# Low parts of weights kept in DRAM after their first use and loaded for the second

## The chip, the cores and the metric

The kernel runs on one core of a Trainium2 chip. The core has a matrix engine (TensorE, PE in the rows; its weight loads are PEld), VectorE (DVE), ScalarE (ACT), GpSimd (POOL) and SyncE (SP), which here only issues DMA transfers (SPq). They work side by side and wait for one another by semaphores. The metric is the time on the device in microseconds (us), smaller is better.

## The reference

One step of a hybrid decoder layer over 1088 token columns: 1024 of a prompt and 64 of samples (8 sequences of 8 tokens), with width 1024, in fp32. Cut to what matters:

```python
h = rms_norm(x, g1)
z = h @ w_in                      # 1024 -> 3*512 + 2*256 + 256 columns
y = concat(rwkv7(z[:1536]), rg_lru(z[1536:2048]), s5(z[2048:]))
x = x + y @ w_out
q = rms_norm(x, g2) @ wq          # cross-attention, 4 heads, 256 memory tokens
x = x + attend(q, mem @ wk, mem @ wv) @ wo
x = x + swiglu(rms_norm(x, g3))   # hidden 2816
y = rms_norm(x, gf)
```

Here `rwkv7` is a recurrence over tokens with a 64 x 64 state for each of 8 heads, `rg_lru` a gated linear recurrence behind a short convolution, and `s5` a linear recurrence with complex states.

## The kernel before, in words

**Products in two parts.** Both operands of a large product are split into a high part (rounded to the matmul's format, fp32r) and a low part (what the rounding left off). `mm3` (L173 to L179) makes three matmuls for each block of 128 of the depth: high weight by high input (L177), high weight by low input (L178), low weight by high input (L179).

**Weights.** `load_w` (L145) brings one tile of 128 x 1024 numbers (512 KB) into `wr`; `wsplit` (L150) has ACT write the high part `wh` (L75, the helper `act`) and POOL subtract it from the raw tile, which gives the low part `wl` (L81, the helper `tt`):

```python
    hi = wp.tile(shape, F32R, name="wh", tag="wh")
    lo = wp.tile(shape, F32R, name="wl", tag="wl")
    act(hi, raw)
    tt(lo, raw, f32(hi), OP.subtract, G)
```

The pool `wp` has two buffers each for `wr`, `wh` and `wl`, so a tile's load waits until the tile two before it has been used up.

**Halves of the columns.** The columns are worked in two parts, `hf` 0 (576 columns, the samples among them) and `hf` 1 (512 columns). The 16 tiles of `w_in` that belong to the RWKV and RG-LRU branches (0 to 15) are loaded and split for half 0 in `zmix` (L750) and `lru` (L865, L922), and loaded and split again for half 1. Tiles 16 and 17 (S5) serve both halves in one go. The 8 tiles of `wo` are loaded in `project` (L1375), which `w_o` (L1538) calls for each half.

**What lies beside them.** Half 0 of `w_in` runs from about us 100 to 340. Half 1 lies at us 340 to 640, mixed with the recurrence of RWKV for half 0 (`Chunks`: chunk states `SV`, matmuls `pp` and `ch`, the triangular inverse with `Wu`, `Xu` and `tm`), whose operands go through DRAM (`ar`, `bk`, `inv_d`, `inv_e` and others). `w_o` of half 0 lies in the stretch 640 to 1094, `w_o` of half 1 at 1094 to 1149, with norm work of half 0 for the SwiGLU blocks beside it on DVE (`late_norm`: `h`, `bt`, `bl`, `b`). The SwiGLU blocks take the rest, from 1149 to 1904; their first weights (`in_w_up`) come into `wX` buffers that older work must leave first.

**Order.** All transfers are issued from one engine (`ld = nc.sync.dma_start`, SP), in one order; one that must wait for its buffer holds back all that stand behind it. Sections with a priority (`pr`) and a scheduler that goes by its own model of times set the order of the instructions on each engine, once, when the program is built; the engines then follow it.

Of the kernel before, what the change touches and what calls it, by code (L numbers as in the profile page):

```python
# [7 lines left out]
F32 = mybir.dt.float32  # L8
F32R = mybir.dt.float32r
# [5 lines left out]
P = 128  # L15
# [40 lines left out]
def body(tc, I, O, dbg=None):  # L56
# [7 lines left out]
    def pool(name, stack, side=None, space=None, bufs=1):  # L64
        kw = dict(name=name, bufs=bufs)
        if space is not None:
            kw['space'] = space
        if space != DRAM:
            kw['reuse_waits'] = "tile"
        if side is not None:  # L70
            kw['side'] = side
        return stack.enter_context(tc.tile_pool(**kw))

    def act(out, in_, f=AF.Copy, **kw):
        return S.activation(out, in_, f, **kw)  # L75
# [4 lines left out]
    def tt(out, a, b, op, eng=None):  # L80
        return (eng or V).tensor_tensor(out, a, b, op=op)  # L81
# [6 lines left out]
    def f32(ap):  # L88
        return ap.bitcast(F32)
# [11 lines left out]
    ld = nc.sync.dma_start  # L101

    cst = pool("cst", es)
    dram = pool("dram", es, space=DRAM)
    wp = pool("wp", es, bufs=2)
# [36 lines left out]
        G.memset(kc[:, i:i + 1], x)  # L142
    k_rms, k_gn, k_ln30, k_tiny, k_hpi, k_zero = (kc[:, i:i + 1] for i in range(6))

    def load_w(ap, shape=(P, 8, P)):  # L145
        raw = wp.tile(list(shape), F32, name="wr", tag="wr")
        ld(raw, ap)
        return wsplit(raw, list(shape))

    def wsplit(raw, shape):  # L150
        hi = wp.tile(shape, F32R, name="wh", tag="wh")
# [3 lines that stand above are left out]
        return hi, lo  # L155
# [55 lines left out]
    for hf, hp in ((0, hpA), (1, hpB)):  # L211
        w = W[hf] + (8 if hf == 0 else 0) + 1
# [13 lines left out]
    def mmt():  # L226
        return psD.tile([P, 512], F32, name="mm", tag="mm", bufs=2)
# [47 lines left out]
    def win(hf, w, evac):  # L275

        wh, wl = w
        for c0, n in GH[hf]:
            pt = mmt()
            mm3(pt[:, :n], lambda k: (wh[:, k, :], wl[:, k, :]), hx(hf, c0, n), 8)  # L280
            evac(c0, n, min(n, 512 - c0), pt[:, :n], RS[hf][:, 1 + c0:1 + c0 + n])
# [8 lines left out]
    for i, (a, b, mus) in enumerate(LORA1):  # L290
        w = b - a
        raw = load_lora1(i) if i else first_w
# [109 lines left out]
    wh, wl = split_w(2, 0)  # L402
    for hf in range(2):
        for c0, n in NG[hf]:
            pt = smt()
            s = 2 if c0 else 1
# [145 lines left out]
    d = 1  # L552
    while d < P:
        n = [P, 8, d]
# [14 lines left out]
    raw = wp.tile([P, 1024], F32, name="wr", tag="wr")  # L569
# [8 lines left out]
    for hf in range(2):  # L578
        for p in range(4):
            for kind in range(3):  # L580
                t = lp.tile([P, W[hf]], F32, name="wag", tag=("lmu", "wag")[(p + kind) % 2], bufs=2)
                for c0, n in GX[hf]:
                    pt = smt()
                    m = slice(P * p, P * p + P)
# [15 lines left out]
    for m in range(2):  # L600
        w = load_w(I['w_in'][16 + m])
# [16 lines left out]
    def e(name, tag="t"):  # L618
        return ep.tile([P, 592 if tag == 'zb' else 576], F32, name=name, tag=tag, bufs=EB[tag])
# [97 lines left out]
    for hf in range(2):  # L717
        for m in range(2):
            yo = sp.tile([P, W[hf]], F32, name="yo", tag="yo", bufs=2)
            for c0, n in GX[hf]:  # L720
                c = slice(OFF[hf] + c0, OFF[hf] + c0 + n)
                pts = []
                for half in (1, 0):
                    pt = smt()
                    o = 256 * half + P * m
# [14 lines left out]
    def zmix(hf, mt, tag):  # L740
        zb, z = e("zb", "zb"), e("z" + tag, tag)
        if hf:
            V.tensor_copy(zb[:, 0:1], zlast[:, mt:mt + 1])
        else:
            V.memset(zb[:, 0:1], 0.0)
        om, mu = omu[:, mt:mt + 1], v_('mu_rkv', mt)

        def ev(c0, n, m, pt, rs):
            tt(zb[:, 1 + c0:1 + c0 + n], pt, rs, OP.mult)
        win(hf, load_w(I['w_in'][mt]), ev)  # L750
        act(z[:, :512], zb[:, 1:513], AF.Copy, scale=om)
        if hf == 0:
            act(bview(z[:, 512:576]), sview(zb[:, 513:585]), AF.Copy, scale=om)
        stt(z[:, :512], zb[:, :512], mu, z[:, :512], OP.mult, OP.add)
        if hf == 0:
            V.tensor_copy(zlast[:, mt:mt + 1], zb[:, 512:513])
            zs = bview(z[:, 512:576])
            stt(zs, zb[:, 513:585].rearrange("p (b t) -> p b t", t=9)[:, :, 0:8], mu, zs, OP.mult, OP.add)
        return z[:, :W[hf]]
# [91 lines left out]
    def lru(hf, m):  # L851
        w = W[hf]
# [8 lines left out]
        def evac_x(c0, n, k, pt, rs):  # L861
            tt(ext[:, 3 + c0:3 + c0 + k], pt[:, :k], rs[:, :k], OP.mult)
            if n > k:
                tt(exs[:, :, 3:11], sview(pt[:, k:]), sview(rs[:, k:]), OP.mult)
        win(hf, load_w(I['w_in'][12 + m]), evac_x)  # L865
        if hf:
            ld(O['conv'][m, :, 0, :], ext[:, 512:515])
        else:
# [19 lines left out]
        s, ns = sp4[:, m:m + 1], nsp4[:, m:m + 1]  # L888
# [29 lines left out]
        def evac_g(c0, n, k, pt, rs):  # L918
            tt(gz[:, c0:c0 + k], pt[:, :k], rs[:, :k], OP.mult)
            if n > k:  # L920
                tt(bview(gz[:, 512:576]), sview(pt[:, k:]), sview(rs[:, k:]), OP.mult)
        win(hf, load_w(I['w_in'][14 + m]), evac_g)  # L922
        gz = gz[:, :w]
        act(gz, gz, AF.Gelu_apprx_tanh)
        tt(gz, gz, hs, OP.mult)
# [446 lines left out]
                stt(h, X[self.hf][:, kt, lo:hi], v_(gname, kt), rs, OP.mult, OP.mult)  # L1372
                put(kt, h)

    def project(w, src, hf, evac, behind=None):  # L1375

        for mt in range(8):
            wh, wl = load_w(w[mt])
            for c0, n in GX[hf]:
                pt = mm_[0]()  # L1380
                mm3(pt[:, :n], lambda k: (wh[:, k, :], wl[:, k, :]),
                    lambda k: (src[k][0][:, c0:c0 + n], src[k][1][:, c0:c0 + n]), 8)
                if behind:
                    behind()
                evac(mt, c0, n, pt[:, :n])
# [62 lines left out]
    OA = [None, None]  # L1448
# [77 lines left out]
    late_norm = []  # L1526

    def w_o(hf):


        nm = Norm(hf)
        put = residual(hf, nm)

        def ev(mt, c0, n, pt):
            put(mt, c0, n, pt)
            if c0 + n == W[hf]:
                ld(x_d[hf][:, mt], X[hf][:, mt])
        project(I['wo'], OA[hf], hf, ev, late_norm.pop(0) if late_norm else None)  # L1538
        return nm

    def slot(hf, i, name):
# [564 lines left out]
```

## Time and profile before

| what | value |
|---|---|
| time, median of 3 runs (lowest to highest) | 1897.87 us (1897.86 to 1900.61) |
| profiled execution, own time | 1905.55 us |
| its span from first to last instruction | 1903.4 us |
| granted TensorE clock, mean over the span | 0.961 of full speed |
| busy: PE, DVE, ACT, POOL | 1780.8, 1108.9, 786.6, 696.0 us (94%, 58%, 41%, 37%) |
| HBM read, written | 170.47 MB, 56.23 MB |

The span is the profiled execution alone, and 2.2 us of its time lie around it. Busy time counts each engine's instructions by themselves, so the shares add up to more than 100%. The shares are means over stretches that have different limits. The chain that ended last is followed back from the last instruction to what released it at each step; where it stays on one engine, no other engine was waited for.

### The profile page before, as it was taken

The page shows a single profiled execution, that of the slowest core. Times are in us where ns is not written, and L with a number is a line of the kernel's source. Part 1 is how long each engine was busy: PE and PEld are TensorE (multiplying, and loading weights), DVE is VectorE, ACT ScalarE, POOL GpSimd, SP SyncE. Part 2 cuts the span into 40 slices and gives each one's busy share as a digit, 9 for nine tenths or more (in the row PEclk, how much of TensorE's full clock was granted, in tenths as well). Part 3 has the DMA queues.
Part 4 walks back from the last instruction along what each step waited for, and adds up shares of the span by engine and source line. Part 5 has one row for each costly group of instructions (what it writes and reads, how often), then busy time and mean ns, then how long its engine had stood idle before and what let it go on. Part 6 is the DMA issues. An engine that isn't in the chain of part 4 may idle for free.

```text
span 1903.4 us, 34672 instructions
## 1 busy us (share of the span) xinstructions
PE 1780.8 (94%) x13664; PEld 1617.9 (85%) x13664; DVE 1108.9 (58%) x2273; ACT 786.6 (41%) x1460; POOL 696.0 (37%) x513
## 2 busy tenths in 40 slices
PE   6998888998998889999999989999999999999997
PEld 6877887777877778897887968999999999999997
DVE  7763767797779454746755588633333333744435
ACT  8542443453434533534554355433333333311114
POOL 3311323434443423232221344744444443422235
PEclk9999998798999979999999998999999999999998
DMA  5037465436564743236553333322222223723102
GB/s 165 30 114 147 123 158 145 138 96 177 152 160 128 233 144 91 67 123 232 170 188 117 115 129 102 117 74 80 80 74 74 86 77 97 272 92 92 56 1 95
DMA packets 192146, 228.95 MB, mean 120 GB/s; under 512 B 80048, under 2 KB 128560, under 8 KB 191568
## 3 DMA queue, kind: packets, MB, share of 16 engines
q1 hardware_dynamic: 191984, 226.75, 39.4%
q8 instruction: 107, 1.75, 0.4%
q14 instruction: 55, 0.45, 0.1%
HBM read 170.47 MB, written 56.23 MB: 119 GB/s over the span
## 4 chain that ended last, share of the span: by engine, by line
PE 62%; DVE 12%; DMA 5%; ACT 2%; issue 2%; POOL 1%; SPq 1%; DVEq 0%; ACTq 0%; POOLq 0%
PE mm L177 17%; PE mm L179 17%; PE mm L178 17%; DMA AR<-ar 1%; PE pp L1052 1%; DVE bl L81 1%; DVE tm L81 1%; DVE Wu L81 1%; DVE Y L78 1%; DVE h L78 1%; DMA fg<-g 1%; DVE X L81 1%; PE ss L1499 1%; ACT L75 1%; PE ch L1124 1%
## 5 line engine op out<-in xcount | busy, mean ns | idle before, releaser
L81 POOL TENSOR_TENSOR wl<-wr,wh 128x1024 fp32r<-128x1024 f32 x104 | 257.5, 2477 | 459.0 <-ACT wh L75 413.3
L177 PE MATMUL mm<-HH,wh 128*128 128x256 f32 (+2 forms) x576 | 180.0, 313 | 11.8 <-DVE gz L81 4.6
L81 DVE TENSOR_TENSOR X<-X,mm 128x288 f32<-128x288 f32 (+2 forms) x200 | 100.5, 512 | 137.3 <-PE mm L179 136.4
L179 PE MATMUL mm<-gh,dl 128*128 128x288 f32 (+2 forms) x560 | 178.5, 319 | 0.0
L177 PE MATMUL mm<-gh,dh 128*128 128x288 f32 (+2 forms) x560 | 178.2, 318 | 0.0
L178 PE MATMUL mm<-gl,dh 128*128 128x288 f32 (+2 forms) x560 | 178.1, 318 | 0.0
L179 PE MATMUL mm<-HH,wl 128*128 128x256 f32 (+2 forms) x576 | 176.5, 307 | 0.0
L178 PE MATMUL mm<-HL,wh 128*128 128x256 f32 (+2 forms) x576 | 175.0, 304 | 0.0
L178 PE MATMUL mm<-bl,st 128*128 128x256 f32 (+1 forms) x596 | 172.2, 289 | 2.6 <-DVE bl L81 2.6
L75 ACT ACTIVATE wh<-wr 128x1024 fp32r<-128x1024 f32 (+1 forms) x105 | 110.3, 1051 | 154.4 <-PE mm L178 74.9
L179 PE MATMUL mm<-bh,st 128*128 128x256 f32 (+1 forms) x596 | 172.1, 290 | 0.6 <-POOL st L81 0.6
L177 PE MATMUL mm<-bh,st 128*128 128x256 f32 (+1 forms) x596 | 171.2, 289 | 0.8 <-ACT bh L75 0.7
L177 PE MATMUL mm<-bh,X 128*128 128x256 f32 (+1 forms) x580 | 165.7, 288 | 0.6 <-DVE p L81 0.5
L178 PE MATMUL mm<-bl,X 128*128 128x256 f32 (+1 forms) x580 | 166.2, 287 | 0.0
L179 PE MATMUL mm<-bh,X 128*128 128x256 f32 (+1 forms) x580 | 165.5, 287 | 0.0
L81 DVE TENSOR_TENSOR gy<-gy,mm 128x288 f32<-128x288 f32 (+1 forms) x130 | 56.7, 436 | 164.9 <-PE mm L179 164.5
L177 PEld LDWEIGHTS mm<-HH,wh 128*128 128x128 f32 x576 | 114.6, 199 | 20.0 <-issue 10.6
L81 POOL TENSOR_TENSOR dl<-wr,dh 128x512 fp32r<-128x512 f32 x44 | 64.6, 1503 | 163.5 <-ACT dh L75 143.4
L178 PEld LDWEIGHTS mm<-HL,wh 128*128 128x128 f32 x576 | 114.7, 199 | 5.1 <-issue 2.8
L179 PEld LDWEIGHTS mm<-HH,wl 128*128 128x128 f32 x576 | 114.5, 199 | 4.4 <-issue 2.2
L178 PEld LDWEIGHTS mm<-bl,st 128*128 128x128 f32 x596 | 113.3, 190 | 2.8 <-DVE bl L81 2.8
L179 PEld LDWEIGHTS mm<-bh,st 128*128 128x128 f32 x596 | 113.4, 190 | 0.8 <-POOL st L81 0.8
(498 smaller groups left out, 5125.1 us busy)
## 6 DMA issues: line engine op xcount, KB each, us to landing
wr<-in_w_in SPq DMA_DIRECT2D x34, 512.0 KB, 4.0
wX<-in_w_up SPq DMA_DIRECT2D x56, 256.0 KB, 2.7
wr<-in_w_down SPq DMA_DIRECT2D x22, 512.0 KB, 4.1
wr<-in_w_out SPq DMA_DIRECT2D x16, 512.0 KB, 4.7
wr<-in_wq SPq DMA_DIRECT2D x16, 512.0 KB, 3.5
kvb<-in_ck SPq DMA_DIRECT2D x32, 256.0 KB, 4.5
kvb<-in_cv SPq DMA_DIRECT2D x32, 256.0 KB, 4.6
wr<-in_wo SPq DMA_DIRECT2D x16, 512.0 KB, 3.5
```

The source lines that it names most:

```text
L75: return S.activation(out, in_, f, **kw)
L78: return V.scalar_tensor_tensor(out, a, s, b, op0=o0, op1=o1)
L81: return (eng or V).tensor_tensor(out, a, b, op=op)
L177: paced(TE.matmul(out, wh, xh, start=first and k == 0, stop=False, **kw))
L178: paced(TE.matmul(out, wh, xl, start=False, stop=False, **kw))
L179: paced(TE.matmul(out, wl, xh, start=False, stop=last and k == n - 1, **kw))
L1052: mi = TE.matmul(pvs[h][:, i, j], BK[o, i, j].rearrange("p a t -> p (a t)"), AR[o, i, h, j].rearrange("p a t -> p (a t)"), start=True, sto ...
L1124: mi = TE.matmul(ch[OWN[h], 0, i], AR[:, i, h, j, 0, :], SV[:, i, h, j, :], start=i == 0, stop=True, skip_group_check=True)
L1499: TE.matmul(sc[32 * h:32 * h + 32, :256], qp[:, 2 * h + dt, :], kb[:, dt, :], start=dt == 0, stop=dt == 1)
```

## The change

`load_w` takes a key. The first load of a tile with a key makes both parts as before, and the low part is then stored to a DRAM buffer of its own by a transfer of 512 KB. The second load of the same key brings the raw tile, has ACT make the high part, and loads the low part from that buffer by another transfer of 512 KB; the subtraction on POOL is not made. Keys are given to the 16 tiles of `w_in` and the 8 tiles of `wo`. So 24 subtractions on POOL go, and 24 stores and 24 loads are added, 12.6 MB each way, all issued by SP. From `load_w` on, line numbers are up to 12 higher than before.

```diff
--- before.py
+++ after.py
@@ -142,10 +142,22 @@
         G.memset(kc[:, i:i + 1], x)
     k_rms, k_gn, k_ln30, k_tiny, k_hpi, k_zero = (kc[:, i:i + 1] for i in range(6))
 
-    def load_w(ap, shape=(P, 8, P)):
+    lows = {}
+
+    def load_w(ap, shape=(P, 8, P), key=None):
+
         raw = wp.tile(list(shape), F32, name="wr", tag="wr")
         ld(raw, ap)
-        return wsplit(raw, list(shape))
+        if key in lows:
+            hi, lo = (wp.tile(list(shape), F32R, name=n, tag=n) for n in ("wh", "wl"))
+            act(hi, raw)
+            ld(f32(lo), lows.pop(key))
+            return hi, lo
+        hi, lo = wsplit(raw, list(shape))
+        if key:
+            lows[key] = dram.tile(list(shape), F32, name="lo_%s%d" % key)
+            ld(lows[key], f32(lo))
+        return hi, lo
 
     def wsplit(raw, shape):
         hi = wp.tile(shape, F32R, name="wh", tag="wh")
@@ -747,7 +759,7 @@
 
         def ev(c0, n, m, pt, rs):
             tt(zb[:, 1 + c0:1 + c0 + n], pt, rs, OP.mult)
-        win(hf, load_w(I['w_in'][mt]), ev)
+        win(hf, load_w(I['w_in'][mt], key=('in', mt)), ev)
         act(z[:, :512], zb[:, 1:513], AF.Copy, scale=om)
         if hf == 0:
             act(bview(z[:, 512:576]), sview(zb[:, 513:585]), AF.Copy, scale=om)
@@ -862,7 +874,7 @@
             tt(ext[:, 3 + c0:3 + c0 + k], pt[:, :k], rs[:, :k], OP.mult)
             if n > k:
                 tt(exs[:, :, 3:11], sview(pt[:, k:]), sview(rs[:, k:]), OP.mult)
-        win(hf, load_w(I['w_in'][12 + m]), evac_x)
+        win(hf, load_w(I['w_in'][12 + m], key=('in', 12 + m)), evac_x)
         if hf:
             ld(O['conv'][m, :, 0, :], ext[:, 512:515])
         else:
@@ -919,7 +931,7 @@
             tt(gz[:, c0:c0 + k], pt[:, :k], rs[:, :k], OP.mult)
             if n > k:
                 tt(bview(gz[:, 512:576]), sview(pt[:, k:]), sview(rs[:, k:]), OP.mult)
-        win(hf, load_w(I['w_in'][14 + m]), evac_g)
+        win(hf, load_w(I['w_in'][14 + m], key=('in', 14 + m)), evac_g)
         gz = gz[:, :w]
         act(gz, gz, AF.Gelu_apprx_tanh)
         tt(gz, gz, hs, OP.mult)
@@ -1372,10 +1384,10 @@
                 stt(h, X[self.hf][:, kt, lo:hi], v_(gname, kt), rs, OP.mult, OP.mult)
                 put(kt, h)
 
-    def project(w, src, hf, evac, behind=None):
+    def project(w, src, hf, evac, behind=None, name=None):
 
         for mt in range(8):
-            wh, wl = load_w(w[mt])
+            wh, wl = load_w(w[mt], key=name and (name, mt))
             for c0, n in GX[hf]:
                 pt = mm_[0]()
                 mm3(pt[:, :n], lambda k: (wh[:, k, :], wl[:, k, :]),
@@ -1535,7 +1547,7 @@
             put(mt, c0, n, pt)
             if c0 + n == W[hf]:
                 ld(x_d[hf][:, mt], X[hf][:, mt])
-        project(I['wo'], OA[hf], hf, ev, late_norm.pop(0) if late_norm else None)
+        project(I['wo'], OA[hf], hf, ev, late_norm.pop(0) if late_norm else None, 'o')
         return nm
 
     def slot(hf, i, name):
```

The first place is SP's order in `w_o` of half 1, before: `wr<-in_wo` are raw tiles of `wo` (the last is tile 7), `wX` are buffers for the SwiGLU weights, `x` the stores of the result.

```order
L1776 DMA wX<-in_w_up 128x512
L1537 DMA x_3543<-X 128x512
L147 DMA wr<-in_wo 128x1024
L1537 DMA x_3543<-X 128x512
L147 DMA wr<-in_wo 128x1024
L1776 DMA wX<-in_w_up 128x512
L1537 DMA x_3543<-X 128x512
L147 DMA wr<-in_w_up 128x1024
L1776 DMA wX<-in_w_up 128x512
```

The same place with the change, where `lo_o_...` are the DRAM buffers of the low parts, the last (11116) that of tile 7, the one before (11049) that of tile 6:

```order
L1788 DMA wX<-in_w_up 128x512
L1549 DMA x_3575<-X 128x512
L154 DMA wl<-lo_o_10982 128x1024
L150 DMA wr<-in_wo 128x1024
L1549 DMA x_3575<-X 128x512
L1788 DMA wX<-in_w_up 128x512
L154 DMA wl<-lo_o_11049 128x1024
L150 DMA wr<-in_w_up 128x1024
L1549 DMA x_3575<-X 128x512
L154 DMA wl<-lo_o_11116 128x1024
L1788 DMA wX<-in_w_up 128x512
L150 DMA wr<-in_w_up 128x1024
```

The load of a low part stands behind the load of its raw tile, and between the two stand, for tiles 6 and 5, stores of `x`, the next raw tile or a `wX` load.

The second place is SP's order ahead of the first chunk of half 0, where the recurrence's operands `BK` and `AR` are read back from DRAM, before:

```order
L147 DMA wr<-in_w_in 128x1024
L846 DMA bv_114<-zz 128x576
L962 DMA Xu<-inv_d_2059 128x1024
L870 DMA out_conv<-exs 128x8x3
L995 DMA Xs<-sd_d 64x64
L1033 DMA BK<-bk_110 128x4x128
L1035 DMA AR<-ar_108 64x4x128 x2
L1036 DMA vt<-v_112 128x4x64
```

With the change, with low parts of `w_in` (`lo_in_...`):

```order
L150 DMA wr<-in_w_in 128x1024
L154 DMA wl<-lo_in_2079 128x1024
L150 DMA wr<-in_w_in 128x1024
L858 DMA bv_114<-zz 128x576
L154 DMA wl<-lo_in_2155 128x1024
L882 DMA out_conv<-exs 128x8x3
L974 DMA Xu<-inv_d_2059 128x1024
L1007 DMA Xs<-sd_d 64x64
L1045 DMA BK<-bk_110 128x4x128
L1047 DMA AR<-ar_108 64x4x128 x2
```

Two low parts and one more raw tile have come ahead of the `AR` loads, and stay in the same queue.

The third place is POOL's order about us 500, where `zk` is made from `f` for the operands of half 1, before:

```order
L86 TENSOR_SCALAR sg<-sg 128x512
L86 TENSOR_SCALAR f<-ta,drv 128x512
L81 TENSOR_TENSOR wl<-wr,wh 128x1024
L81 TENSOR_TENSOR zk<-zk,f 128x512
L81 TENSOR_TENSOR sp_4827<-SV,pcs_148 64x128 x2
L81 TENSOR_TENSOR hat<-BK,pcs_148 128x512
```

With the change:

```order
L86 TENSOR_SCALAR sg<-sg 128x512
L86 TENSOR_SCALAR f<-ta,drv 128x512
L81 TENSOR_TENSOR zk<-zk,f 128x512
L81 TENSOR_TENSOR sp_4907<-SV,pcs_148 64x128 x2
L81 TENSOR_TENSOR hat<-BK,pcs_148 128x512
```

The subtraction that stood between `f` and `zk` is gone.

## Rows read from the trace of the kernel before

**Rows 1.** Busy time by stretch: PE, PEld, DVE, ACT, POOL, granted clock, DMA share, GB/s.

```profile
340.00:640.00 300.00, 274.90 (x2474) 226.95 (x2473) 240.73 (x499) 133.79 (x210) 125.99 (x102) 0.90 0.54 150
...
1094.00:1149.00 55.00, 48.69 (x207) 38.79 (x206) 44.88 (x68) 28.69 (x42) 23.50 (x8) 0.97 0.39 133
```

**Rows 2.** Groups of POOL by tile: busy us, mean ns, idle before, releasers.

```profile
L81 POOL TENSOR_TENSOR wl<-wr,wh 128x1024 fp32r<-128x1024 f32 x103 | 256.2, 2488 | 457.0 <-ACT wh L75 411.2 <-ACT wsm L75 14.3 <-PE sc L178 6.3
```

**Rows 3.** Timeline of DVE, us 388 to 393: start, duration, operation.

```profile
390.36 0.43 DVE L81 TENSOR_TENSOR zb<-mm,RS 128x256 f32<-128x256 f32 x1
390.70 2.20 DVE L81 TENSOR_TENSOR tm<-Xu,Wu 128x247 f32<-128x247 f32 x1
392.93 0.42 DVE L81 TENSOR_TENSOR Wu<-Wu,tm 128x247 f32<-128x247 f32 x1
```

**Rows 4.** Timeline of POOL in the same stretch.

```profile
390.24 2.39 POOL L81 TENSOR_TENSOR wl<-wr,wh 128x1024 fp32r<-128x1024 f32 x1 [2.74 <-ACT wh L75]
```

**Rows 5.** Chain that ended last, us 340 to 640: start, duration, piece.

```profile
345.46 9.24 DMA AR<-ar
...
390.79 2.12 DVE tm L81
...
416.30 2.25 DMA fg<-g
...
465.18 2.78 DVE zz L78
468.62 2.73 DVE ta L78
...
567.92 2.45 DVE tm L81
...
583.90 2.31 DVE Wu L81
...
592.77 2.75 DVE Y L81
...
621.72 2.96 DMA inv_e<-Wu
```

**Rows 6.** Timeline of DVE, us 503 to 507.

```profile
504.35 0.75 DVE L78 SCALAR_TENSOR_TENSOR kk<-zk,vec,nr 128x512 f32<-128x512 f32 x1 [3.53 <-ACT nr L75]
```

**Rows 7.** Timeline of POOL, us 497 to 512.

```profile
505.64 2.40 POOL L81 TENSOR_TENSOR wl<-wr,wh 128x1024 fp32r<-128x1024 f32 x1 [5.04 <-ACT wh L75]
507.99 1.29 POOL L81 TENSOR_TENSOR zk<-zk,f 128x512 f32<-128x512 f32 x1
```

**Rows 8.** Waits of PE, us 1095 to 1152: us in total, times, longest.

```profile
PE mm L179 <- POOL wl L81: 6.3, 3, 3.3
```

**Rows 9.** Timeline of PE in that stretch, matmuls of w_o half 1.

```profile
1126.98 0.50 PE L179 MATMUL mm<-oh,wl 128*128 128x512 f32 x1 [2.34 <-POOL wl L81]
...
1141.55 0.50 PE L179 MATMUL mm<-oh,wl 128*128 128x512 f32 x1 [3.29 <-POOL wl L81]
...
1142.35 0.39 PE L179 MATMUL mm<-oh,wl 128*128 128x512 f32 x1
...
1143.23 0.63 PE L179 MATMUL mm<-oh,wl 128*128 128x512 f32 x1
```

**Rows 10.** DMA issues (KB, median us to landing), 1048 to 1110; 340 to 365 with GB/s.

```profile
wr<-in_wo SPq DMA_DIRECT2D x9, 512.0 KB, 3.4
...
GB/s 413 297 354 11 13 131 269 361 93 5 1 1 8 25 76 27 40 32 88 234 304 296 221 377 406 419 284 342 390 361 400 383 410 243 59 26 26 13 0 0
...
wr<-in_w_in SPq DMA_DIRECT2D x2, 512.0 KB, 8.3
```

**Rows 11.** The same view, us 240 to 270.

```profile
wr<-in_w_in SPq DMA_DIRECT2D x3, 512.0 KB, 5.8
```

**Rows 12.** Chain that ended last, us 1090 to 1160.

```profile
1136.00 1.05 ACT wh L75
```

**Rows 13.** Timeline of the DMA queue on SP, w_o half 1.

```profile
1131.81 0.33 SPq L1776 DMA_DIRECT2D wX<-in_w_up  x1
```

**Rows 14.** Waits of ACT, us 100 to 340, for raw weight tiles.

```profile
ACT wh L75 <- DMA wr<-in_w_in: 7.4, 1, 7.4
```

## The prediction

> **What bounds the kernel now.** I read busy time by stretch first, since the change touches only the stretches in which a keyed tile is used, and takes work away only where it is used the second time. In the stretch of half 1 of `w_in` (340 to 640) PE is busy 274.90 of 300 us, DVE 240.73, POOL 125.99, at a granted clock of 0.90 [rows 1]. So PE idles 25.1 us there, and no saving by other engines can give much more than that, apart from what a higher clock returns. In the 55 us of `w_o` half 1 PE is busy 48.69, so 6.3 us can be had [rows 1]. Then the POOL groups: the subtraction for `wl` runs 103 times at 2.488 us [rows 2]; the change drops 24, about 60 us of POOL's work. That is no time by itself, because POOL is the bound nowhere. What counts is whom a subtraction holds up, and for that I went to the chain that ended last, to PE's waits and to the timelines of DVE and POOL.
>
> **What is removed.** Three effects.
>
> First, DVE beside a subtraction. At 390.70 DVE's `tm`, which reads two buffers of SBUF, took 2.20 us; `Wu`, of the same shape, took 0.42 right behind it. A subtraction on POOL ran from 390.24 for 2.39 us, and `tm` ended when it did; `zb`, which reads PSUM, took only 0.43 beside it [rows 3, 4]. So a DVE operation with two inputs in SBUF stands still while a subtraction runs. The Trainium skill says the same (SBUF — State Buffer, Who interferes with whom: such an operation and a GpSimd instruction that reads SBUF exclude each other for a whole instruction); by it alone 24 subtractions would free DVE of up to 24 x 2.4 = 58 us, an estimate. What is worth something is only what the chain shows. In 340 to 640 it has eight DVE pieces of this kind beside subtractions that go: 2.12, 1.67, 2.49 (two operations), 2.78, 2.73, 2.45, 2.31, 2.75, together 19.3 us, from `tm` at 390.79 to `Y` at 592.77; six of the eight pieces are shown [rows 5]. Unblocked, the three of `tm` and `Wu` would take 0.42 [rows 3] and the other six operations at most 0.75, as `kk` does [rows 6]: 1.3 + 4.5 = 5.8. So 13.5 us of excess lie on the chain. Bounds: nothing (other work lies right behind, and the scheduler orders anew) and 13.5 (all of it). I take half, 6.8, because PE is 92% busy here: when a DVE operation ends 2 us earlier, what is waited for next is often work that is still in PE's queue; no row says which end is nearer.
>
> Second, POOL's order. The subtraction at 505.64 stands ahead of `zk`, which starts only at 507.99 [rows 7]; `zk` can start once `kk` has read its old content, at 504.35 + 0.75 = 505.10 [rows 6]. It would come 2.9 us earlier, and it is on the chain's way. Bounds 0 and 2.9; I take half, 1.5, for the same reason.
>
> Third, `w_o` half 1. PE waits there three times for a `wl`, 6.3 us in all [rows 8]; two of them, 2.34 and 3.29, come before a matmul of tiles 5 and 7 [rows 9]. After the second one, matmuls took 0.63 us, where 0.39 is usual, for 3 us: some 1.6 us lost [rows 9]. Together 2.34 + 3.29 + 1.6 = 7.2.
>
> **What is added.** A low part now needs a transfer. Alone, 512 KB land 3.4 us after issue; in the crowded stretch 340 to 365 it takes 8.3 [rows 10], in 240 to 270 it takes 5.8 [rows 11]. The way that goes, ACT (1.05, [rows 12]) and POOL (2.4, [rows 2]), takes 3.5 us from the buffer's release, so with nothing in front of it the load is no later than the subtraction; it is later only where something stands ahead of it on SP or on the DMA engines.
>
> In `w_o` half 1 something does. In the new order the low part of tile 6 stands behind the third `wX` load. That one was issued at 1131.81 in the trace, when its buffer came free [rows 13]; then the low part lands no sooner than 1131.81 + 0.4 + 3.4 = 1135.6, and the tile's first low matmul was due at 1133. So 2.6 us are lost there, and what DVE does for half 0 (which releases the `wX` buffers) sets it. Net of 7.2: 4.6. Bounds: 7.2, if the `wX` buffers come free earlier now that DVE is blocked less, and -1.0, if the low part of tile 5 behind the second `wX` load is as late too and more is lost in clock (2 x 2.6 + 3 against 7.2).
>
> In front of the first chunk, two low parts come into the queue ahead of `AR`, which took 9.24 us on the chain at 345.46 [rows 5]. At some 400 GB/s, which most busy slices of that stretch move [rows 10], 512 KB are 1.3 us, so two are 2.6 later. Bounds 0 (they have landed before) and 4.9 (8.3 less 3.4).
>
> Behind it the chain has further transfers of the recurrence, from `fg` at 416.30 (2.25) to `inv_e` at 621.72 (2.96) [rows 5], seven in all. Sixteen low parts of 3.4 us in 300 us cover 0.18 of the time; each of the seven would be 1.3 late in a fifth of cases: 1.8, say 2. Bounds 0 and, if each were 2.4 late (5.8 less 3.4, [rows 10, 11]), 16.8.
>
> The stores in the first pass go at nothing: ACT waited only once for a raw tile of `w_in` in 100 to 340, for 7.4 us [rows 14], so raw tiles are early there, and a store of 3.4 us delays a load that has that cover. Without the cover it would be one store for that one wait, 3.4 us at most; nobody else waits for a store.
>
> **Sum**, against the span 1903.4 of the profiled execution: -6.8 - 1.5 - 4.6 + 2.6 + 2 = -8.3, so 1895.1. The profiled execution took 1905.55, 7.7 above the median of the three runs, 1897.87; the same 8.3 off the median gives 1889.6, so **1890**.
>
> **The rivals.** *Full relief* (chance 0.13): DVE's delays carry through in full, since blocked operations off the chain also come earlier; then -13.5 - 2.9 - 7.2 + 2 = -21.6, about 1876 (1871 to 1882). For it: 13.5 of excess are on the chain now. Against it: PE has only 25 + 6.3 us idle in both stretches, so two thirds of it would have to go.
>
> *Nothing* (0.21): the chain runs from PE to PE, and each relief ends at the next wait for PE or a transfer, which come as late as before; 1894 to 1902, which is also what this kernel's measurement can't tell from no change (0.2%, 3.8 us). For it: PE's 92%.
>
> *Slower by transfers* (0.22): the chain's eight transfers between 340 and 640 each land 2.4 later, as three loads of 512 KB close together do (5.8 for 3.4, [rows 10, 11]), because 16 more loads of 512 KB share the engines and the queue of SP: 8 x 2.4 = 19.2, against 12.9 of relief (6.8 + 1.5 + 4.6), so +6.3, 1904; without the gain in `w_o` +11, 1909. It ends on the slow side from 2.1 us for each of the eight ((12.9 + 3.8) / 8). For it: DMA's share is 0.54 already [rows 1], and a held transfer on SP holds all behind it. Against it: most recurrence transfers stand alone. The Trainium skill (DMA: Bandwidth & Descriptors, Latency and other measured facts) has access to HBM take 0.2 us on average and 2 us at high load; 3.4 against 8.3 here agrees in direction. By its figures it would be 1.8 for each of eight, 14 us, an estimate, and so not slower by more than can be told.
>
> *The forecast* (0.44): 1882 to 1894.
>
> **How the numbers follow.** Faster by over 0.2% takes the forecast and full relief, 0.57; within 0.2% 0.21; slower 0.22. The range leaves out half of full relief (below 1875) and the upper part of the slower case (above 1904): 0.07 + 0.12, which leaves 0.81. The forecast's own range is 1882 to 1894.
>
> **What would show it.** Right: no PE wait for a `wl` from POOL in `w_o` half 1, but one of 2 to 3 us for the low part of tile 6; POOL's busy time lower by about 60 us; DVE's busy time in 340 to 640 lower by 25 or more, with `zz`, `ta` and `tm` at 0.4 to 0.8 on the chain; PE's idle time there down from 25 to about 20; `AR` about 2.6 longer on the chain. Wrong: PE's idle time in 340 to 640 as before or larger, with waits for `AR`, `bk`, `inv_d` or a `wl` load in front of it, or SP held at a low part that waits for its buffer while operands of the recurrence stand behind it; or a first pass in which ACT waits more often for raw tiles because stores stand in the way.

## The result, and the profile after

The changed kernel takes 1880.44 us (median of 4 runs, 1877.89 to 1882.63); the kernel before takes 1897.95 (4 runs). The ratio is 0.9901, interval 0.9882 to 0.9919: 18.8 us faster by the ratio, 15.4 to 22.4. Forecast were 8.3 us. The direction was right and the time lies in the range (1875 to 1904), but the gain is more than twice the forecast, and it lies in the band of the rival "full relief" (1871 to 1882).

The profile after, the page's busy times (share of the span, instructions):

```profile
span 1876.5 us, 34713 instructions
## 1 busy us (share of the span) xinstructions
PE 1769.1 (94%) x13664; PEld 1612.6 (86%) x13664; DVE 1075.7 (57%) x2273; ACT 786.1 (42%) x1461; POOL 632.1 (34%) x489
```

POOL lost 63.9 us for 24 operations, as expected; DVE lost 33.2 us without losing one of its 2273 operations. That is the first sign of the mechanism: the same DVE work ran faster. The two stretches that answer to [rows 1], by the same columns; the second is `w_o` half 1, from its first matmul to the first of the SwiGLU blocks:

```profile
340.00:640.00 300.00, 279.58 (x2530) 233.11 (x2529) 216.88 (x506) 134.75 (x212) 91.54 (x89) 0.89 0.65 183
...
1075.60:1122.30 46.70, 46.11 (x204) 37.66 (x204) 34.01 (x68) 28.53 (x42) 2.41 (x1) 1.00 0.70 234
```

In `w_o` half 1, 55.0 us have become 46.7, PE idles 0.6 us, and the granted clock is at full (1.00 for 0.97). In 340 to 640 more matmuls fit into the same 300 us (2530 for 2474), with DVE at 216.88 for 240.73. DMA's share rose from 0.54 to 0.65.

POOL's group that answers to [rows 2], and DVE's timeline in a piece of `w_o` half 1:

```profile
L81 POOL TENSOR_TENSOR wl<-wr,wh 128x1024 fp32r<-128x1024 f32 x79 | 192.8, 2441 | 417.8 <-ACT wh L75 383.3 <-ACT wsm L75 16.9 <-PE sc L190 6.3
```

```profile
1096.36 0.94 DVE L78 SCALAR_TENSOR_TENSOR h<-X,vec,acc 128x288 f32<-128x288 f32 x2
1097.22 0.68 DVE L81 TENSOR_TENSOR X<-X,mm 128x512 f32<-128x512 f32 x1
1097.82 0.45 DVE L81 TENSOR_TENSOR bt<-h,bt 128x288 f32<-128x288 f32 x1
1098.18 0.45 DVE L81 TENSOR_TENSOR bt<-h 128x288 f32<-128x288 f32 x1
1098.55 0.75 DVE L81 TENSOR_TENSOR bl<-h,bh 128x576 fp32r<-128x576 f32 x1
```

The remaining subtractions take as long as ever. The row to look at is `bt<-h,bt` at 0.45: in the trace of before, one of this shape took 2.07 in this stretch, where `X<-X,mm`, which reads PSUM, took 0.68 as here:

```profile
1109.97 0.68 DVE L81 TENSOR_TENSOR X<-X,mm 128x512 f32<-128x512 f32 x1
1110.57 2.07 DVE L81 TENSOR_TENSOR bt<-h,bt 128x288 f32<-128x288 f32 x1
```

The waits of PE in `w_o` half 1 (in place of [rows 8]), SP's row that answers to [rows 13], and the chain's piece that answers to `AR` in [rows 5]:

```profile
PE mm L191 <- DMA wl<-lo_o: 0.6, 1, 0.6
```

```profile
1105.79 0.33 SPq L1788 DMA_DIRECT2D wX<-in_w_up  x1
1106.21 0.38 SPq L154 DMA_DIRECT2D wl<-lo_o  x1
```

```profile
349.12 8.33 DMA AR<-ar
```

The third `wX` load was issued 37.4 us after the first matmul of this stretch before (1131.81 from 1094.4), and 29.8 after it now (1105.79 from 1076.0). The low part of tile 6 still stands behind it, and PE waits 0.6 us for it, not the 2.6 that were forecast. This `AR` did not become longer. The next one on the chain did; first the trace of before, then that of the change:

```profile
515.81 4.27 DMA AR<-ar
```

```profile
511.68 6.93 DMA AR<-ar
```

**Where the time went.** For each matmul that has the same line, operands and rank in two traces I took the difference of its start times. The table has the median of these differences in six stretches (named by the times of before), in us; negative is earlier than in the trace of before. Each row is one profiled execution, and two of the same kernel, `e0_before` and the one shown ahead of the prediction, differ by up to 2.4 in these stretches and by up to 5 between them (430 to 440, 580 to 600).

| kernel | end of w_in half 0 (320-340) | 440-460 | 600-620 | 760-790 | before w_o half 1 (1070-1090) | behind it (1180-1200) |
|---|---|---|---|---|---|---|
| before, second profile (e0_before) | 2.0 | -2.4 | -1.2 | -0.0 | -0.9 | -0.8 |
| the change | 3.1 | 2.2 | -7.5 | -14.5 | -18.4 | -26.8 |
| subtraction back on POOL (e3_poolback) | 3.1 | 6.1 | -11.2 | -16.5 | -14.1 | -14.0 |
| work of the change, order of before (f1) | 6.6 | 0.1 | -8.8 | -12.1 | -12.4 | -22.5 |
| order of before, no subtraction, no transfer (f5) | 0.4 | -2.5 | -13.1 | -12.9 | -13.4 | -23.0 |
| order of the change, no transfer (f4) | 4.1 | 2.5 | -9.5 | -19.0 | -22.7 | -32.3 |

The change loses 3 us in half 0 of `w_in`, gains some 17 us between 440 and 790, 4 more up to 1070, and 8.4 in `w_o` half 1. The 3 us are not the stores' here: f4, which stores nothing, is as late. The 4 us may belong to the one execution of before, since `e0_before` drifts from it by 3.3 about 1020 and is within 0.9 of it again at 1070. Behind 1180 nothing more moves. The profiles are 26.9 us apart and the medians 17.5: the profiled executions of before (1905.55, and 1904.63 for the second) are longer than its median, so sizes below come from the timed runs and the table tells only where.

### The profile page after: what moved, and what is told of

Read it like the earlier page. It is cut to its first block, busy times and chain, and to the rows that moved or that the text cites. A ratio compares the mean times of both kernels' runs of the same rounds, so it can differ in the third digit from the quotient of the medians.

```text
span 1876.5 us, 34713 instructions
## 1 busy us (share of the span) xinstructions
PE 1769.1 (94%) x13664; PEld 1612.6 (86%) x13664; DVE 1075.7 (57%) x2273; ACT 786.1 (42%) x1461; POOL 632.1 (34%) x489
## 4 chain that ended last, share of the span: by engine, by line
PE 61%; DVE 11%; DMA 6%; ACT 2%; issue 2%; POOL 1%; SPq 1%; DVEq 0%; ACTq 0%; POOLq 0%
PE mm L190 17%; PE mm L189 17%; PE mm L191 17%; DMA AR<-ar 1%; PE pp L1064 1%; DVE Y L78 1%; DVE tm L81 1%; DMA fg<-g 1%; DVE bl L81 1%; DVE Wu L81 1%; DMA wr<-in_w_out 1%; DVE X L81 1%; ACT L75 1%; PE ch L1245 1%; DVE hql L78 1%
## 5 line engine op out<-in xcount | busy, mean ns | idle before, releaser
L81 POOL TENSOR_TENSOR wl<-wr,wh 128x1024 fp32r<-128x1024 f32 x80 | 194.0, 2426 | 419.9 <-ACT wh L75 385.4
```

## The experiments

Each was timed in 5 rounds beside the kernel before (`e0_before` in 3); ratios are of these. Microseconds gained or lost are the ratio's distance from 1 times 1898, where no two medians are named.

### Which half of the change, and is it the subtraction on POOL?

**e0_before.** 

> The kernel before once more, for a second profile of it. Its first profiled execution took 1905.55 us, 7.7 above its median. If 8 of the 27 us between the two profiles are only that execution, this profile's span is near 1896, and its stretch from 340 to 700 is the shorter one; if its time is as long again with a profile, the span is near 1903 and the difference of the profiles holds as it stands. Time: 1898.

1899.4 us, ratio 1.0005 (0.999 to 1.0021); the span of its profile is 1902.5, and its rows for the two stretches read as in [rows 1]:

```profile
340.00:640.00 300.00, 273.61 (x2462) 226.74 (x2460) 243.82 (x498) 134.30 (x209) 128.94 (x100) 0.90 0.54 150
1093.00:1148.00 55.00, 48.67 (x206) 38.77 (x206) 44.78 (x68) 28.61 (x42) 23.48 (x8) 0.97 0.40 132
```

Profiled executions of this kernel are long ones, and the busy times come again. Which DVE operations are caught beside a subtraction does not: of the eight pieces of [rows 5] that the prediction counted, four stand on this profile's chain again at the same length (`tm` at 390, `thi`, `zz`, `ta`), and `tm`, `Wu` and `Y` at 568 to 593 take 0.38, 0.41 and 0.68 here, while other operations near them take 2.5.

**e1_win** and **e2_wo**, with keys at one part alone:

```diff
# e1_win
-        project(I['wo'], OA[hf], hf, ev, late_norm.pop(0) if late_norm else None, 'o')
+        project(I['wo'], OA[hf], hf, ev, late_norm.pop(0) if late_norm else None)
# e2_wo
-        win(hf, load_w(I['w_in'][mt], key=('in', mt)), ev)
+        win(hf, load_w(I['w_in'][mt]), ev)
```

(and so for the other two loads of `w_in`).

> Keys for the 16 tiles of w_in alone; wo is split on POOL both times, as before. Theory A (DVE and POOL were held by subtractions in half 1 of w_in, and more of it carries through than the half that was forecast): 10 to 11 us faster than before, 1887 to 1888. Rival B (the sum of the prediction for w_in was right, 3.7 us, and the rest lies in wo): 1894 to 1895.

> Keys for the 8 tiles of wo alone. Theory A: the whole gap of PE in w_o half 1 goes (55 to 46.7 us in the profiles), 8 us faster, 1890. Rival B: more than that, 14 to 15 us, 1883 to 1884, since the rest of the gain has to be here. The prediction's own sum: 4.6 us, 1893.

`w_in` alone: 1888.09, ratio 0.9949 (0.9931 to 0.9968), 9.7 us faster. `wo` alone: 1889.92, ratio 0.9967 (0.9952 to 0.9981), 6.3 us faster by the ratio, and in its profile `w_o` half 1, from its first matmul's start to its last one's end, takes 47.1 us for 54.3. Together 16 of the 18.8: the two parts add up within their intervals, and both times are near theory A.

**e3_poolback**, the change, but POOL subtracts again and nobody uses the result:

```diff
             ld(f32(lo), lows.pop(key))
+            tt(raw, raw, f32(hi), OP.subtract, G)
             return hi, lo
```

> The change as it is, but at the second use POOL makes the subtraction once more, in place on the raw tile, for nobody: the transfers stay, wl comes from DRAM, and only POOL's time and what it holds up (DVE operations with two inputs in SBUF, and what stands behind it on POOL) come back. Theory A (that is what the w_in part gained): the 10 us of w_in are lost again and some of wo's 8 stay, 1888 to 1892, with DVE pieces of 2 to 3 us on the chain again. Rival C (the gain comes from the other order of the instructions and from wl no longer waiting for POOL): 1880 to 1883, as with the change.

1889.96, ratio 0.9959 (0.9946 to 0.9973): 11 of the 18.8 us are gone again, though no matmul waits for this subtraction. DVE (first) and POOL (second) of this run in one place, and the waits of PE in `w_o` half 1:

```profile
399.84 2.58 DVE L81 TENSOR_TENSOR Wu<-Wu,tm 128x247 f32<-128x247 f32 x1
...
402.45 0.42 DVE L81 TENSOR_TENSOR tm<-Xu,Wu 128x252 f32<-128x252 f32 x1
```

```profile
399.66 2.49 POOL L81 TENSOR_TENSOR wr<-wr,wh 128x1024 f32<-128x1024 f32 x1 [10.21 <-ACT wh L75]
```

```profile
PE mm L192 <- DMA wl<-lo_o: 4.7, 2, 2.4
```

`Wu` takes 2.58 us beside the subtraction, `tm` 0.42 behind it. `w_o` half 1 takes 54.9 us, as long as before, though all its low parts come from DRAM: with DVE blocked again the third `wX` load is issued 37.5 us into the stretch (1118.55 from 1081.0), as in the trace of before, and two low parts on SP behind `wX` loads come 2.4 us late. That is what the prediction feared, and it happens only while DVE is blocked.

**e4_memset**, POOL busy as often, but only writing:

```diff
             ld(f32(lo), lows.pop(key))
+            for h in range(2):
+                G.memset(raw, float(h))
             return hi, lo
```

> As the run before with POOL busy for nobody, but POOL only writes: two memsets of the raw tile (about 1 us each in the trace of before) in place of the subtraction, which reads two buffers. Theory A1 (what the subtractions cost is that a DVE operation with two inputs in SBUF stands still while POOL reads SBUF): the change's gain stays, 1880 to 1883, and DVE pieces beside the memsets keep their 0.4 to 0.8 us. Theory A2 (what counts is POOL's queue, the work behind a subtraction): 1887 to 1890, as with the subtraction.

1880.98, ratio 0.9895 (0.9873 to 0.9916), as the change itself. DVE and POOL of this run:

```profile
404.43 0.42 DVE L81 TENSOR_TENSOR Wu<-Wu,tm 128x256 f32<-128x256 f32 x1
...
405.44 0.42 DVE L81 TENSOR_TENSOR tm<-Xu,Wu 128x255 f32<-128x255 f32 x1
```

```profile
404.26 1.97 POOL L156 MEMSET wr<- 128x1024 f32 x2 [9.89 <-ACT wh L75]
```

The same DVE operations take 0.42 beside 1.97 us of POOL writing. DVE's busy time says the same over whole runs: 1105 to 1116 us in the five with the 24 subtractions (before, e0_before, e3, e5 and f2, below), 1071 to 1077 in the five without (the change, e4, f1, f4, f5), whatever their order. So what slows DVE is that POOL reads SBUF while DVE wants its second input from there. That this, and not POOL's queue, makes up the time (theory A1) is what 1881 against 1890 says. The raw tile's buffer is not the reason either: between 340 and 640 SP waits 13.3 us for POOL to release it in e4 and 12.7 in e3. The Trainium skill (SBUF — State Buffer, Who interferes with whom) says that such a DVE instruction contends with a GpSimd instruction that reads SBUF, not with one that only writes; 2.58 against 0.42 agree. Two reserves: two memsets take 1.97 us and a subtraction 2.5, so POOL was held a little less; and each of these two runs has an order of its own, as the next section shows, so not all of the 9 us between them need be the cause's. The runs in one order below bear it out in part.

### What do the transfers cost? Runs that the scheduler put in order anew

**e5_stores**:

```diff
-        if key in lows:
+        if key in lows and False:
...
-        if key:
+        if key and key not in lows:
```

> The first use stores the low part to DRAM, the second use splits the tile on POOL as before: the 24 stores alone. The prediction put them at nothing; in the profile of the change the program stands 3 us later at the end of half 0 of w_in than before. If the stores do that: 1901, 3 us slower than before. If it is other (order, one execution's clock): 1898.

1904.91, ratio 1.0021 (1.0 to 1.0042): between nothing and 8 us, which leaves both cases open.

**e6_nolow** (the store is left out too):

```diff
-            hi, lo = (wp.tile(list(shape), F32R, name=n, tag=n) for n in ("wh", "wl"))
+            hi = wp.tile(list(shape), F32R, name="wh", tag="wh")
             act(hi, raw)
-            ld(f32(lo), lows.pop(key))
-            return hi, lo
+            return hi, hi
```

> At the second use neither a subtraction nor a transfer: the matmuls that want the low weight take the high one (so the low part of these weights is left out of the product, and its place is taken by the high part), and nothing is stored. PE's work is the same. It shows what the whole relief is worth without any transfer. If transfers cost what the prediction said (2.6 for AR, 2 for others) and the stores 3: 1872 to 1873. If the transfers are hidden: 1880, as with the change.

1866.15, ratio 0.9822 (0.98 to 0.9845): 34 us faster than before, more than either theory.

**e7_all**:

```diff
-        project(I['w_out'], Y, hf, residual(hf, nm))
+        project(I['w_out'], Y, hf, residual(hf, nm), name='out')
...
-        project(I['wq'], hq, hf, ev, lambda: first and first.pop()())
+        project(I['wq'], hq, hf, ev, lambda: first and first.pop()(), 'q')
```

> Keys for w_out and wq too, 40 tiles in place of 24. In half 1 of these PE is busy 97% with the change, and PE waits for no wl there, so a gain is bounded by some 10 us of idle time in 390 us: 1876 to 1880 if DVE's relief counts there as well, 1880 to 1883 if it is hidden or the added transfers cost as much.

1887.04, ratio 0.9936 (0.9914 to 0.9958), 6.6 us slower than the change. Both theories miss. Whether 16 more loads and stores or the order did it was not told apart.

**e8_actq**, **e9_loads**, **e10_poolstore**:

```diff
# e8_actq, e10_poolstore
-            ld(f32(lo), lows.pop(key))
+            nc.scalar.dma_start(f32(lo), lows.pop(key))
# e10_poolstore
-            ld(lows[key], f32(lo))
+            nc.gpsimd.dma_start(lows[key], f32(lo))
# e9_loads
+    seen = set()
...
-        if key in lows:
+        if key in seen:
...
-            ld(f32(lo), lows.pop(key))
+            ld(f32(lo), lows[key])
...
+            seen.add(key)
-            lows[key] = dram.tile(list(shape), F32, name="lo_%s%d" % key)
-            ld(lows[key], f32(lo))
+            if not lows:
+                lows[key] = dram.tile(list(shape), F32, name="lo_%s%d" % key)
+                ld(lows[key], f32(lo))
+            lows[key] = next(iter(lows.values()))
```

> The change, but the loads of the low parts are issued from ACT, right behind the operation that makes the high part, in place of SP. Bytes and transfers are the same. In the profile of the change SP is held 9 times, 37.4 us in all, at a low part that waits for its buffer, with the recurrence's operands behind it. Theory Q (what the loads cost, some 11 of the 15 us by which the run without low parts is faster than the change, is this hold on SP): 1869 to 1874. Rival D (it is the DMA engines' time, with 8 MB more in this stretch): 1879 to 1882, as with the change.

> The change with 2 stores in place of 24: only the first tile of each weight is stored, and every second use loads that one (so the low parts of the other tiles are wrong). All 24 loads stay on SP. If the stores cost the 3 to 4 us that the run with stores alone and the landmarks at 340 show: 1876 to 1877. If stores are hidden: 1880.

> Loads of low parts issued from ACT, as two runs above, and the stores from POOL, right behind the subtraction that makes the part. If the stores cost what they do because they hold SP until POOL is done: 3 us better than with the loads on ACT alone, 1866 to 1871 under theory Q, 1876 to 1878 under D. If the stores' cost is the DMA engines' time, or POOL's way of issuing a transfer costs DVE or POOL more than SP's: no better than with the loads on ACT alone, or worse.

e9_loads as run makes one store, not two: the first tile of `w_in`, and every second use loads that part. Loads from ACT 1870.29 (0.9858, 0.9836 to 0.988); one store 1860.37 (0.9804, 0.9782 to 0.9827); stores from POOL besides 1883.12 (0.9934, 0.9911 to 0.9958). Taken at their word these would say that stores cost 20 us, though stores alone cost 4, and that the run with 24 loads and one store is faster than the one without any transfer. They contradict each other, and each has an order of its own: the scheduler goes by its model, and every edit gives it other times. In the traces, DVE's sequence departs from that of the change somewhere between the 300th and the 600th of its 2273 operations in e3 to e6 and e8 to e10, and near the 1050th in e7. So the next runs hold the order.

### The same work in one order

Each engine's order is taken from a built kernel and held by dependencies that only order and never wait, chained along the list of each engine:

```diff
+def in_order(tc):
+    import array, base64, zlib
+    ins = [i for i in tc.nc.cur_bb.bb.instructions if type(i).__name__ != "BassTilePoolBoundary"]
+    last = {}
+    for k in array.array("H", zlib.decompress(base64.b85decode(ORDER))):
+        i = ins[k]
+        e = str(i.engine)
+        if e in last:
+            tc.add_manual_dep(i, last[e].name, NOSYNC, reason="order")
+        last[e] = i
...
         body(tc, I, O)
+        in_order(tc)
```

`f1` is the changed kernel and `f2` the kernel before, each with `ORDER` from the other; `f4` and `f5` are e6_nolow with the order of the change and of before. Their matmuls are as many as before, at the same granted clock in 340 to 640 (0.91 and 0.90, for 0.90 before).

> All work of the change (24 stores, 24 loads, no subtraction at the second use), but every engine's order is held to that of the kernel before by a chain of order-only dependencies (no waits): each load of a low part stands on SP where the order of before has the operation that makes the high part, each store some 25 instructions behind its subtraction. If the whole gain of 18.8 us is the work (relief less transfers): 1879 to 1882. If it is the scheduler's new order: 1898. Half and half: 1889.

> The other corner: the work of the kernel before (subtraction on POOL at the second use, no stores and loads of low parts), each engine's order held to that of the change. If the gain is the work: 1898 or more, since the order was made for other work. If it is the order: 1880. Half and half: 1889.

> The order of the change, held; no subtraction, no store and no load at the keyed uses, the high part is taken in place of the low one (so the product lacks these low parts). Against the change it takes away the transfers alone. If transfers cost 15 us, as the run of this kind in its own order says (1866): 1864 to 1867. If they are nearly free and that run's order was the reason: 1877 to 1880.

> The order of the kernel before, held; the 24 subtractions of the second use are left out and nothing is loaded in their place (the high part is taken for the low one, so the product lacks these low parts). Against the kernel before it takes away the subtractions alone, in the same order: what they cost. By the prediction's sum of reliefs 12.9 us: 1885; by its upper bounds 23.6 us: 1874; by the run of this kind in its own order 34 us: 1864.

| | order of before | order of the change |
|---|---|---|
| work of before | 1898.0 (the kernel before) | 1896.25, 0.9998 (0.9985 to 1.0012) |
| work of the change | 1879.92, 0.9905 (0.9892 to 0.9918) | 1880.44, 0.9901 (the change) |
| no subtraction, no transfer | 1873.79, 0.9874 (0.9853 to 0.9894) | 1870.21, 0.9851 (0.9836 to 0.9866) |

Down a column, the order is one and only the work differs. The whole gain is work: the order of the change gives nothing to the work of before (0.4 us), and the work of the change gives 18.0 in the order of before. In that order the 24 subtractions cost 23.9 us (20 to 28), and the transfers that take their place cost 5.9 back; in the order of the change it is 28 and 9.5. In `w_o` half 1 the stretch is 45.4 us in both runs in the order of before, with transfers and without (54.3 before): 8.9 us are the subtractions', and the transfers cost nothing there. The row of that stretch with the work of the change in the order of before (f1):

```profile
1082.00:1128.00 46.00, 46.00 (x206) 37.72 (x205) 34.08 (x68) 28.91 (x42) 2.42 (x1) 1.00 0.72 237
```

These runs also show DVE in one order. In f5 the operations that stood still in the trace of before have their usual length; `tm` took 2.20 there [rows 3], `zz` and `ta` 2.78 and 2.73 on the chain [rows 5]:

```profile
392.24 0.41 DVE L81 TENSOR_TENSOR tm<-Xu,Wu 128x247 f32<-128x247 f32 x1
...
462.80 0.73 DVE L78 SCALAR_TENSOR_TENSOR zz<-zb,vec,zz 128x512 f32<-128x512 f32 x1
...
464.11 0.68 DVE L78 SCALAR_TENSOR_TENSOR ta<-ta,Pi 128x512 f32<-128x512 f32 x1
```

And POOL's `zk` starts 0.9 us behind the start of DVE's `kk`, which it waits for, where it stood 3.6 behind it before [rows 6, 7]. First DVE, then POOL:

```profile
500.73 0.75 DVE L78 SCALAR_TENSOR_TENSOR kk<-zk,vec,nr 128x512 f32<-128x512 f32 x1 [3.53 <-ACT nr L75]
```

```profile
501.64 1.30 POOL L81 TENSOR_TENSOR zk<-zk,f 128x512 f32<-128x512 f32 x1 [5.02 <-DVE kk L78]
```

By the method of the table above, in steps of 10 us, PE of f5 against the trace of before gains 3.8 us between 380 and 430, 1.1 between 450 and 480 (`zz`, `ta`), nothing between 500 and 530 (`zk`), and 9.8 between 560 and 610. Against `e0_before`, the last is 8.7. So the 2.7 us by which POOL's queue was shorter at `zk` did not reach PE. Nor is it that a `wl` comes sooner: PE waited only 1.0 us for one of POOL's in 340 to 640 before.

**Which transfers.** `f3` is e9_loads and `f6` is e8_actq, both in the order of the change.

> The order of the change, held; one store in place of 24, and all 24 loads bring that one low part (so the other low parts are wrong). Without any transfer this order took 1870, with all of them 1880. If the stores are what costs: 1871 to 1873. If it is the loads: 1878 to 1880. Half each: 1875.

> The change in its own order, held, but the 24 loads of low parts are issued from ACT behind the operation that makes the high part. The same on ACT in an order of its own took 1870. If it was the hold on SP that went: 1871 to 1874 here as well. If that run's other order was the reason: 1879 to 1882.

One store: 1881.98, ratio 0.9913 (0.9896 to 0.9929), so 23 stores less change nothing that can be measured in this order, and it is the loads that cost: this run and f4 differ in 24 loads and one store, and by 11.8 us. Loads from ACT: 1878.89, ratio 0.9909 (0.9891 to 0.9926), no better than from SP. So taking the hold off SP wins nothing, though SP is held at low parts in the change and not in this run. First the waits of the DMA queue on SP from 340 to 610 in the change, then those of the run with loads from ACT:

```profile
SPq L154 <- PE mm L191: 37.4, 9, 11.7
```

```profile
SPq L1048 <- PE pp L1091: 19.4, 5, 4.8
SPq L1674 <- ACT wh L75: 16.5, 2, 13.9
```

37.4 us of hold at low parts are gone, and the time is the same. Some of the hold has moved, not gone: in this run ACT waits 3.6 us and PE 2.2 for a low part, and neither does in the change. So that the hold itself cost nothing is not shown.

By elimination the loads' time on the DMA engines remains; the rows for it are weak. First the run in this order without transfers, then the one with 24 loads and one store, raw tiles of `w_in` in 340 to 610 (KB each, median us to landing):

```profile
wr<-in_w_in SPq DMA_DIRECT2D x14, 512.0 KB, 4.4
```

```profile
wr<-in_w_in SPq DMA_DIRECT2D x14, 512.0 KB, 5.0
```

In the order of before it is 5.0 without any transfer (f5, the row below) and 5.3 with all of them (f1), so the order alone moves this figure as much:

```profile
wr<-in_w_in SPq DMA_DIRECT2D x13, 512.0 KB, 5.0
```

The Trainium skill (DMA: Bandwidth & Descriptors, Issuing engines are not separate DMA queues) says that transfers from every issuing engine share the same 16 DMA engines, which agrees with ACT being no better than SP. Matmul by matmul, the one-store run falls behind the run without transfers in three places (by the times of before), by 3.7 us between 420 and 460, 2.7 between 500 and 530 and 4.7 between 600 and 640. In the second of them the `AR` transfer on the chain lasts 6.02 us without loads and 7.14 with them:

```profile
511.71 6.02 DMA AR<-ar
```

```profile
514.16 7.14 DMA AR<-ar
```

That is 1.1 of the 11.8 us. By what the others reach the end stays open.

**A faster version.** 

> All work of the change (24 stores, 24 loads, nothing left out) in the order that the scheduler made for the run with one store, which took 1860; the 23 other stores are put some 25 instructions behind their subtractions. If that order is the better one: 1862 to 1870, faster than both kernels. If the stores make up the difference: 1878 to 1882.

1864.83, ratio 0.9841 (0.9816 to 0.9867): 30 us faster than before and 15.6 faster than the change by the medians (11.4 by the ratios), with all of the change's work. The same 24 loads and one store took 1860 in the order made for them and 1882 in that of the change. And the loads from ACT took 1870 in the order made for them and 1879 in that of the change. So what made e8 and e9 look so good was their order. Why this order is the better one was not looked into.

## Why the prediction was right or wrong

- **DVE stands still beside a subtraction: right.** It was read from one pair of rows [rows 3, 4]. In one and the same order the operations that stood still take their usual time once the subtraction is gone (f5), and a POOL that only writes leaves them alone (e4). That the time follows DVE and not POOL's queue rests on e3 (1890) and e4 (1881), each in an order of its own, and on `zk` in f5, where a shorter queue gained nothing.
- **"I take half, 6.8": this step failed.** The DVE excess of 13.5 us came through as a whole, not by half. In the order of before, without subtractions, the gain is 23.9 us (20 to 28), of which 8.9 lie in `w_o` half 1; the other 15.0 stand against 6.8 + 1.5 = 8.3 as taken. Piece by piece it is less even, as far as single profiles tell. The excess in the sum was 3.6 at the first three pieces, 4.0 at `zz` and `ta` and 5.9 at the last three, and PE of f5 gained 3.8, 1.1 and 8.7 to 9.8 there. The last three were not even caught in `e0_before`, though other operations near them were. So which operations stand still is partly chance, while DVE's busy time in 340 to 640 is much the same (240.73 and 243.82). The reason given for half, PE busy 92%, was no measurement of the path: PE's busy share says how much idle time there is (25.1 us), not that a delay on the chain ends in PE's queue.
- **POOL's order, 1.5 of 2.9: did not come.** `zk` came 2.7 us earlier relative to `kk` in f5, and PE gained nothing between 500 and 530.
- **`w_o` half 1, 4.6: mis-sized.** It measured 8.4 in the change and 8.9 in the order of before. The gross sum of 7.2 was low: it left out the third wait of [rows 8], 0.7 us, and more was lost in slow matmuls than the 1.6 put down. The 2.6 taken off it did not come: the third `wX` load was issued 7.6 us earlier in the stretch, because DVE, which releases its buffer, was no longer blocked (SP waited 14.5 us for DVE's `h` there before, 4.4 in the change). The prediction named this as the reason for its upper bound and then took the other end. Both ends occurred, the late one in e3_poolback, where DVE is blocked: two waits of 2.4.
- **Transfers, 2.6 + 2 = 4.6: the sum near, the parts wrong.** They cost 5.9 in the order of before and 9.5 in that of the change, each give or take some 5. The first `AR` took 8.33 for 9.24 on the chain, so its 2.6 are not there. The second took 6.93 for 4.27, but 6.02 without any transfer in the same order, so most of that is the order's. Where the rest of the cost arises is open.
- **Stores at nothing: right within what was measured.** One store in place of 24 in the order of the change is 2.3 us slower by the ratios, inside the intervals. Half 0 of `w_in` ends as late without stores (f4, 4.1) as with them (3.1). In the order of before the profiles differ there, 6.6 late with stores (f1) and 0.4 without (f5); no run in that order has the loads alone, so it stays open.
- **Rivals.** "Full relief" (0.13) was the case: 21.6 forecast, 18.8 measured, and 23.9 less 5.9 by the runs in one order. "Nothing" fell with e1 and e2. "Slower by transfers": 12.6 MB each way cost 6 to 10 us, not 19. SP held at low parts with the recurrence behind, which was named as a sign of being wrong, did occur (37.4 us), and taking it away gained nothing.

With the bounds in place of the halves the prediction's sum would have been 13.5 + 2.9 + 7.2 - 4.6 = 19.0, against 18.8. That it meets so well is partly luck: the 2.9 did not come, `w_o` gave more than 7.2 and the transfers cost more than 4.6.

## What to carry to other kernels

The busy share of the main engine is no reason to halve an excess that stands on the chain: here the sum of the excess came whole (3.8 + 1.1 + 8.7 or more, for 13.5), though single pieces gave more or less. A second profile of the same kernel tells which pieces are chance. A late transfer is priced with the buffer release that holds it, and the release moves with the same change. When a scheduler orders anew, compare work in one held order first: here the same work was 9, 16 and 22 us apart in two orders, as much as the change was worth, and in the two orders compared first not apart at all (1879.92 and 1880.44).

## What was not expected of the hardware

A POOL operation that reads SBUF makes a DVE operation with two inputs there wait until it ends (2.58 us for 0.42), and one that writes the same 128 x 1024 buffer in 1.97 us does not slow it at all (0.42). With SP no longer held for 37.4 us at loads that wait for their buffers, the time was the same (1879 for 1880).
